# Forming the low part of B22 first in the 7-product steps of a fused encoder block, with its product first

## The chip, the cores and the metric

The kernel runs on one core of a Trainium2 chip. The metric is the device time of one execution in microseconds (us), as the median of several runs. The profile comes from one further execution, whose own time is given beside its span.

## What is computed

The reference is one layer of a streaming encoder block on 256 tokens of width 4096: a normalised input goes through one wide projection, then through a sparse attention branch and a state-space branch, both come back to 4096 columns, are gated, summed, projected once more, normalised and added to the input.

```python
h = rms_norm(x, pre_norm_gain[layer])
proj = h @ w_in[layer]
...
attn = dsa_attention(q, k, v, qi, ki, wi * idx_weight_scale)
y_a = attn.reshape(b, s, ATTN_WIDTH) * jax.nn.silu(gate_a)
...
merged = (gates[:, :, 0, :] * (y_a @ w_branch_attn[layer])
          + gates[:, :, 1, :] * (y_b @ w_branch_ssd[layer]))
out = merged @ w_out[layer]
x = x + rms_norm(out, post_norm_gain[layer])
```

Nearly all the work is in the matrix products with `w_in`, the two branch weights and `w_out`, and nearly all of these go through one function, `pair_gemm`.

## The kernel before, in words

**How a product is made.** Every float32 operand is split into a high part (rounded to the type that TensorE multiplies in one pass, `F32R`) and a low part (what the rounding left). One product is then three matmuls into the same PSUM tile: low of the activations with high of the weights, high with low, high with high (`product`, line 554, in this order). The activations are the stationary operand and are split beforehand; the weights are the moving operand and are split as they arrive. ScalarE makes the high part (an activation with Copy), VectorE the low part (a subtraction).

**Steps.** `pair_gemm` makes two blocks of 128 tokens by two blocks of 512 columns. It runs over 16 pairs of 128 rows of weights (8 in the branch projections), and each pair is one step of a plan. A step loads the weight blocks B12 and B22 into `ra` and B11 and B21 into `rb`, each block 128 by 512. A step of kind D or R makes eight block products. A step of kind S makes seven, by sums and differences of blocks in the manner of Strassen: the sums on the side of the activations lie ready in `ext`, those on the side of the weights are formed in the step. A DMA with accumulation (line 601) first adds B11 to the first half of `ra`, which gives T1; VectorE then forms T2 = T1 - B22 in the second half of `ra` (line 622) and T3, T4 in `rb` (line 623), over the blocks that were there.

**What an S step puts on the engines.** ScalarE makes five high parts: B11 and B21 together (line 507, 1024 columns), B22 (line 617), T1 (line 619), T2 (line 507, 512 columns), T3 and T4 together (line 507). VectorE makes the five low parts belonging to them (line 511, 618, 625, 511, 511) and the two sums of lines 622 and 623. TensorE makes 21 matmuls, in the order of products 2, 1, 3, 5, 6, 7, 4: products 2 and 1 use B21 and B11, product 3 uses B22, product 5 uses T1, product 6 T2, products 7 and 4 T3 and T4. A step of kind D or R has two high parts and two low parts of 1024 columns, no sums, and 24 matmuls.

**Buffers.** The high parts of 1024 columns live in a pool of four buffers, the low parts in another of four (`SBUFS = 4`). An S step takes three of each, for B11 and B21 (`wh_...` of line 613 before), for B22 and T1 together, and for T3 and T4; the part of T2 has a single buffer of its own. A step of kind D or R takes two. A new high part waits until TensorE has done the last product that reads what was in its buffer.

**What sets the order.** The code is recorded, and a scheduler then puts each engine's instructions into an order by their place in the code, by readiness as it models it, and by free buffers; it also decides which buffer a tile gets. `tc.keep_in_program_order` pins an instruction among the pinned ones of its engine. Each engine works through its own queue in order. Beside the steps, generators (`aux`) put the work of earlier stages (rotary embedding, attention, convolution, the scan, the merging) between them, a few instructions at each `step(pace)`.

The plans name the S steps: nine of 16 in most stages (`SX`, `SM`), seven in the state-space stage (`SS`), ten in the later gate projections (`SG` = 1, 3, 4, 6, 7, 9, 10, 12, 13, 14). An S step thus follows another one at 3-4, 6-7 and 9-10, and in the late gates also at 12-13 and 13-14.

Of the kernel before, what the change touches and what calls it, by code (L numbers as in the profile page):

```python
# [13 lines left out]
AF = mybir.ActivationFunctionType  # L14
# [3 lines left out]
P = 128  # L18
# [3 lines left out]
NW = 512  # L22
# [26 lines left out]
def fused_block(tc, x, xT, w_qi, w_misc, w_q0, w_qk, w_vg, w_x, w_z, w_gate, w_br, w_out2, w_out,  # L49
                percol, rows, tabs, tris, pgain, out):  # L50
    nc = tc.nc
    V, A, G, T = nc.vector, nc.scalar, nc.gpsimd, nc.tensor
# [11 lines left out]
    def bank(j):  # L64
        return pq.tile([P, NW], F32, tag=f"p{j}", name=f"p{j}")
# [8 lines left out]
    def fbit(ap):  # L74
        return ap.bitcast(F32)
# [44 lines left out]
    def drain(upto=None):  # L120
        while aux and (upto is None or upto in aux):
            step()

    def push(gen):
        aux.append(gen)
        return gen
# [18 lines left out]
    def raw_tile():  # L145
        return rawp.tile([P, HK, NW], F32, tag="raw", name="raw")

    def load_half(raw, chunk, hf, each=False):
        if each:
            for i in range(HK):  # L150
                nc.sync.dma_start(raw[:, i, :], chunk[:, hf * HK + i, :])
        else:
            nc.sync.dma_start(raw, chunk[:, hf * HK:(hf + 1) * HK, :])
# [333 lines left out]
    def form(i, name):  # L487
        n = int(name[1])
        if name[0] == "S":
            n = (3, 0, 1, 2)[n - 1]  # L490
            return ext[i][:, 0, n, :], ext[i][:, 1, n, :]
        if name[0] == "D":
            return ext[i][:, 0, n - 1, :], ext[i][:, 1, n - 1, :]
        tk = slice((n - 1) * P, n * P)
        k = int(name[2]) - 1
        return base[i][:, 0, k, tk], base[i][:, 1, k, tk]

    def split_tiles(n):
        if n == 1:
            return (whp.tile([P, 1, NW], F32R, tag="wh1", bufs=1, name="wh"),  # L500
                    wlp.tile([P, 1, NW], F32R, tag="wl1", bufs=1, name="wl"))
        return (whp.tile([P, n, NW], F32R, tag="wh", name="wh"),
                wlp.tile([P, n, NW], F32R, tag="wl", name="wl"))

    def split(src, n, sign=1):
        h, l = split_tiles(n)
        A.activation(h, src, AF.Copy, scale=float(sign))  # L507
        if sign < 0:
            V.scalar_tensor_tensor(l, src, -1.0, fbit(h), ALU.mult, ALU.subtract)  # L509
        else:  # L510
            V.tensor_sub(l, src, fbit(h))  # L511
        return [(h[:, j, :], l[:, j, :]) for j in range(n)]
# [16 lines left out]
    def run_pending():  # L529
        while pending:  # L530
            pending.pop(0)()
# [4 lines left out]
    def pair_gemm(what, mode, chunk, plan, outs, evac, hooks={}, pace=1):  # L536

        while len(live) > 1:
            drain(live.popleft())
        left = {}  # L540
        for _, kind in plan:
            for j, n in USES[kind].items():
                left[j] = left.get(j, 0) + n
        ps = {}
        dest = []

        def product(j, i, name, w):
            (ah, al), (bh, bl) = form(i, name), w
            first = j not in ps
            if first:  # L550
                ps[j] = bank(phys[j])
            left[j] -= 1
            for n, (l, r) in enumerate(((al, bh), (ah, bl), (ah, bh))):
                T.matmul(ps[j], l, r, start=first and n == 0, stop=left[j] == 0 and n == 2)  # L554

        def early():
            dest.extend(outs())
            A.activation(dest[0], ps[1], AF.Copy)
            V.tensor_add(dest[1], ps[6], dest[0])
            V.tensor_add(dest[2], ps[7], dest[1])  # L560

        def late():
            if not dest:
                dest.extend(outs())
                A.activation(dest[1], ps[5], AF.Copy, scale=-1.0)
                return
            V.tensor_add(dest[1], ps[5], dest[1])
            if 8 in ended:
                V.tensor_sub(dest[3], dest[3], ps[5])
                return  # L570
            V.scalar_tensor_tensor(dest[3], ps[5], -1.0, dest[2], ALU.mult, ALU.subtract)

        def rest():
            c11, c12, c21, c22 = dest
            if 1 not in ps:
                A.activation(c11, ps[2], AF.Copy)
                A.activation(c21, ps[4], AF.Copy)
                V.tensor_sub(c22, c12, ps[8])
                V.tensor_sub(c12, c12, ps[3])
                return  # L580
            V.scalar_tensor_tensor(c12, ps[3], -1.0, c12, ALU.mult, ALU.subtract)
            if 8 in ps and 8 not in ended:
                V.tensor_sub(c22, c22, ps[8])
            V.tensor_add(c11, ps[2], c11)
            V.tensor_add(c21, ps[4], c21)

        def end():
            rest()
            live.append(push(evac(dest)))

        after = max([n for n, (_, kind) in enumerate(plan) if kind == "S"], default=-2) + 1
        ended = []
        loaded = deque()

        def fetch(n):
            i, kind = plan[n]
            ra, rb = raw_tile(), raw_tile()
            load_half(ra, chunk(i), 0)
            load_half(rb, chunk(i), 1)
            if kind == "S":  # L600
                nc.gpsimd.dma_start(ra[:, 0, :], chunk(i)[:, HK, :], accum_op=ALU.add)
            loaded.append((ra, rb))

        for n in range(LEAD):
            fetch(n)
        for n, (i, kind) in enumerate(plan):
            if n + LEAD < len(plan):
                fetch(n + LEAD)
            ra, rb = loaded.popleft()
            if n in hooks:  # L610
                hooks[n]()
            assert kind_of[i] == what, (n, i, kind_of, len(aux))
            assert kind == "R" or ext_n[i] == {"S": 4, "D": 2}[kind], (n, i, ext_n)
            if kind == "S":
                b11, b21 = split(rb, 2)
                h, l = split_tiles(2)
                A.activation(h[:, 1, :], ra[:, 1, :], AF.Copy)  # L617
                V.tensor_sub(l[:, 1, :], ra[:, 1, :], fbit(h[:, 1, :]))  # L618
                A.activation(h[:, 0, :], ra[:, 0, :], AF.Copy)  # L619
                if n == 1:  # L620
                    run_pending()
                V.tensor_sub(ra[:, 1, :], ra[:, 0, :], ra[:, 1, :])  # L622
                V.tensor_sub(rb, rb, ra[:, 1:2, :].to_broadcast([P, 2, NW]))  # L623
                tc.keep_in_program_order(
                    V.tensor_sub(l[:, 0, :], ra[:, 0, :], fbit(h[:, 0, :])))  # L625
                t1, b22 = ((h[:, j, :], l[:, j, :]) for j in range(2))
                t2, = split(ra[:, 1:2, :], 1)
                t3, t4 = split(rb, 2)
                now = {1: ("A11", b11), 2: ("A12", b21), 3: ("S4", b22), 4: ("A22", t4),
                       5: ("S1", t1), 6: ("S2", t2), 7: ("S3", t3)}  # L630
                for j in (2, 1, 3, 5, 6, 7, 4):
                    product(j, i, *now[j])
            else:
                w = {}
                w[1, 2], w[2, 2] = split(ra, 2, -1)
                w[1, 1], w[2, 1] = split(rb, 2)
                if n == 0 and len(pending) > 1 and turned[0] == "aux":
                    pending.pop(0)()
                if n == 1:
                    run_pending()  # L640
                if n == after:
                    early()
                    if not left.get(5):
                        late()
                        ended.append(5)
                if n == len(plan) - 1 and dest and not ended and left.get(8) == 0:
                    V.scalar_tensor_tensor(dest[3], dest[2], -1.0, ps[8], ALU.mult, ALU.subtract)
                    ended.append(8)
                todo = [(k, j) for j in ((5, 3, 2, 4) if kind == "D" else (3, 8, 2, 4))
                        for k in (1, 2)]  # L650
                for k, j in todo:
                    name = {2: f"A1{k}", 4: f"A2{k}", 8: f"A2{k}", 5: f"A2{k}",
                            3: f"D{k}" if kind == "D" else f"A1{k}"}[j]
                    product(j, i, name, w[k, 1 if j in (2, 4) else 2])
                    if (k, j) == todo[3]:
                        step(pace)
            step(pace)
        if 5 not in ended:
            pending.append(late)
        pending.append(end)  # L660
        turn(mode)
# [714 lines left out]
```

## Time and profile before

| | |
|---|---|
| median of 3 runs | 2809.67 us (2809.47 to 2812.0) |
| profiled execution: its own time / its span | 2809.73 us / 2808.0 us |
| DVE (VectorE) busy | 2508.4 us, 89% |
| ACT (ScalarE) busy | 1803.2 us, 64% |
| POOL (GpSimd) busy | 220.4 us, 8% |
| S steps (instructions of line 622) | 219 |
| matmuls of line 554 | 10095 |

In the rows of the profile, PE is TensorE's matmul, PEld its weight load, DVE VectorE, ACT ScalarE. A row of the timeline gives start and length in us, engine, line, operation, what is written and read, shapes and count; in brackets stands the idle time of the engine before it and what ended that. Starts are what the argument goes by: instructions that follow each other on one engine overlap at their ends.

### The profile page before, as it was taken

How to read it: one execution, taken by the hardware profiler on the slowest of the kernel's cores; microseconds unless marked ns; L12 is line 12 of the kernel's file. 1: busy time of each engine (PE TensorE's matmuls, PEld its weight loads, DVE VectorE, ACT ScalarE, POOL GpSimd, SP SyncE). 2: the span in 40 equal slices, each digit the busy share in tenths (PEclk: the TensorE clock that was granted, in tenths of full speed). 3: DMA queues.
4: the chain of work that ended last, by engine and by line, in shares of the span. 5: the costliest groups of instructions: out<-in, count | busy, mean ns of one | idle time of the engine just before them, and what ended most of it. 6: DMA issues, size and time to landing. Idle time of an engine off the chain costs nothing.

```text
span 2808.0 us, 36830 instructions
## 1 busy us (share of the span) xinstructions
PE 2782.5 (99%) x12603; PEld 2282.5 (81%) x12603; DVE 2508.4 (89%) x3316; ACT 1803.2 (64%) x2541; POOL 220.4 (8%) x263
## 2 busy tenths in 40 slices
PE   9999999999999999999999999999999999999998
PEld 7877888888888888787888788888888888788886
DVE  7668999999999988989898999999987999989975
ACT  7444566665666666887788866666665655655653
POOL 0100000000000000000000010110110100000000
PEclk9999999999999999999999999999999999999999
DMA  9544777777777777576767788888877888867874
GB/s 375 195 168 143 217 225 228 236 210 222 232 224 232 222 219 231 175 222 202 218 195 211 232 256 251 254 251 255 269 257 246 256 268 270 273 215 235 268 258 142
DMA packets 206333, 649.91 MB, mean 231 GB/s; under 512 B 23232, under 2 KB 24000, under 8 KB 206144
## 3 DMA queue, kind: packets, MB, share of 16 engines
q1 hardware_dynamic: 163728, 567.05, 59.9%
q0 software_dynamic: 33776, 64.77, 13.1%
q10 hardware_dynamic: 8640, 15.73, 1.5%
q8 instruction: 99, 1.62, 0.2%
q14 instruction: 90, 0.74, 0.1%
HBM read 627.53 MB, written 19.92 MB: 231 GB/s over the span
## 4 chain that ended last, share of the span: by engine, by line
PE 93%; DVE 4%; ACT 1%; issue 1%; DMA 0%; SPq 0%; DVEq 0%; ACTq 0%
PE p L554 77%; PE p L205 4%; PE p L206 4%; PE p L207 4%; PE p L377 1%; DVE wl L511 1%; ACT wh L507 1%; DVE raw L623 0%; PE p L408 0%; PE p L921 0%; PE p L786 0%; PE p L753 0%; DVE cacc L857 0%; DVE raw L622 0%; DVE og L1255 0%
## 5 line engine op out<-in xcount | busy, mean ns | idle before, releaser
L507 ACT ACTIVATE wh<-raw 128x1024 fp32r<-128x1024 f32 (+1 forms) x1115 | 1056.6, 972 | 594.5 <-DVE raw L622 251.0
L554 PE MATMUL p<-wh,b 128*128 128x512 f32 x4350 | 1431.8, 393 | 0.6 <-ACT wh L507 0.5
L511 DVE TENSOR_TENSOR wl<-raw,wh 128x1024 fp32r<-128x1024 f32 (+1 forms) x886 | 950.5, 1088 | 69.0 <-ACT wh L507 60.7
L554 PEld LDWEIGHTS p<-wh,b 128*128 128x128 f32 x4350 | 816.6, 188 | 170.6 <-ACT wh L507 3.6
L554 PE MATMUL p<-wl,b 128*128 128x512 f32 x2175 | 848.8, 390 | 0.0
L554 PE MATMUL p<-wh,ext 128*128 128x512 f32 x2380 | 796.8, 390 | 1.5 <-ACT wh L507 1.0
L554 PEld LDWEIGHTS p<-wh,ext 128*128 128x128 f32 x2380 | 446.9, 188 | 94.2 <-ACT wh L507 2.9
L554 PEld LDWEIGHTS p<-wl,b 128*128 128x128 f32 x2175 | 408.8, 188 | 82.6 <-DVE wl L509 0.4
L554 PE MATMUL p<-wl,ext 128*128 128x512 f32 x1190 | 469.1, 394 | 3.6 <-DVE wl L625 3.4
L509 DVE SCALAR_TENSOR_TENSOR wl<-raw,wh 128x1024 fp32r<-128x1024 f32 x229 | 279.1, 1219 | 45.9 <-ACT wh L507 44.9
L554 PEld LDWEIGHTS p<-wl,ext 128*128 128x128 f32 x1190 | 223.4, 188 | 63.3 <-DVE wl L625 11.1
L623 DVE TENSOR_TENSOR raw<-raw 128x1024 f32<-128x1024 f32 x219 | 267.9, 1223 | 5.7
L197 DVE TENSOR_TENSOR wl<-raw,wh 128x1024 fp32r<-128x1024 f32 x112 | 139.8, 1249 | 86.2 <-ACT wh L196 86.0
L617 ACT ACTIVATE wh<-raw 128x512 fp32r<-128x512 f32 x219 | 137.7, 629 | 109.7 <-PE p L554 99.4
L196 ACT ACTIVATE wh<-raw 128x1024 fp32r<-128x1024 f32 x112 | 118.4, 1059 | 136.1 <-PE p L207 119.4
L205 PE MATMUL p<-wh,b 128*128 128x512 f32 x512 | 201.9, 395 | 1.7 <-ACT wh L193 1.7
L206 PE MATMUL p<-wl,b 128*128 128x512 f32 x512 | 200.1, 391 | 0.2 <-DVE wl L194 0.2
L207 PE MATMUL p<-wh,b 128*128 128x512 f32 x512 | 199.8, 391 | 0.0
L618 DVE TENSOR_TENSOR wl<-raw,wh 128x512 fp32r<-128x512 f32 x219 | 150.2, 686 | 18.5 <-ACT wh L617 17.0
L622 DVE TENSOR_TENSOR raw<-raw 128x512 f32<-128x512 f32 x219 | 150.8, 689 | 4.9
L625 DVE TENSOR_TENSOR wl<-raw,wh 128x512 fp32r<-128x512 f32 x219 | 149.7, 684 | 0.0
L619 ACT ACTIVATE wh<-raw 128x512 fp32r<-128x512 f32 x219 | 135.2, 617 | 2.8 <-ACT yraw L381 2.7
(242 smaller groups left out, 1839.2 us busy)
## 6 DMA issues: line engine op xcount, KB each, us to landing
raw<-w_gate_d SPq DMA_DIRECT2D x256, 512.0 KB, 5.8
raw<-w_vg_d SPq DMA_DIRECT2D x128, 512.0 KB, 5.3
raw<-w_x_d SPq DMA_DIRECT2D x128, 512.0 KB, 5.1
raw<-w_br_d SPq DMA_DIRECT2D x128, 512.0 KB, 5.4
raw<-w_out_d SPq DMA_DIRECT2D x128, 512.0 KB, 5.1
raw<-w_qk_d SPq DMA_DIRECT2D x96, 512.0 KB, 5.5
raw<-w_z_d SPq DMA_DIRECT2D x64, 512.0 KB, 5.2
raw<-w_qi_d SPq DMA_DIRECT2D x62, 512.0 KB, 7.7
```

The source lines that it names most:

```text
L197: V.tensor_sub(wl, rs, wh.bitcast(F32))
L205: T.matmul(ps[t], al[:, tk], wh[:, i, :], start=first, stop=False)
L206: T.matmul(ps[t], ah[:, tk], wl[:, i, :], start=False, stop=False)
L207: T.matmul(ps[t], ah[:, tk], wh[:, i, :], start=False, stop=last)
L507: A.activation(h, src, AF.Copy, scale=float(sign))
L509: V.scalar_tensor_tensor(l, src, -1.0, fbit(h), ALU.mult, ALU.subtract)
L511: V.tensor_sub(l, src, fbit(h))
L554: T.matmul(ps[j], l, r, start=first and n == 0, stop=left[j] == 0 and n == 2)
L618: V.tensor_sub(l[:, 1, :], ra[:, 1, :], fbit(h[:, 1, :]))
L622: V.tensor_sub(ra[:, 1, :], ra[:, 0, :], ra[:, 1, :])
L623: V.tensor_sub(rb, rb, ra[:, 1:2, :].to_broadcast([P, 2, NW]))
L625: V.tensor_sub(l[:, 0, :], ra[:, 0, :], fbit(h[:, 0, :])))
```

## The change

In an S step the tiles for B22 and T1 are taken before those for B11 and B21. The high part of B22 and its low part (line 619 now) come first, then the high and low part of B11 and B21 (lines 618 and 620), and then, as before, the sums (625, 627), the low part of T1 (629), of T2 (633), of T3 and T4 (511). Six of VectorE's instructions of the step are pinned where one was: all but the low parts of B22 and of T3 and T4. The products run in the order 3, 2, 1, 5, 6, 7, 4: the product with B22 comes first. Nothing is added or left out: the same five high parts, five low parts, two sums and 21 matmuls.

```diff
             if kind == "S":
-                b11, b21 = split(rb, 2)
                 h, l = split_tiles(2)
+                hb, lb = split_tiles(2)
                 A.activation(h[:, 1, :], ra[:, 1, :], AF.Copy)
+                A.activation(hb, rb, AF.Copy)
                 V.tensor_sub(l[:, 1, :], ra[:, 1, :], fbit(h[:, 1, :]))
+                tc.keep_in_program_order(V.tensor_sub(lb, rb, fbit(hb)))
+                b11, b21 = ((hb[:, j, :], lb[:, j, :]) for j in range(2))
                 A.activation(h[:, 0, :], ra[:, 0, :], AF.Copy)
                 if n == 1:
                     run_pending()
-                V.tensor_sub(ra[:, 1, :], ra[:, 0, :], ra[:, 1, :])
-                V.tensor_sub(rb, rb, ra[:, 1:2, :].to_broadcast([P, 2, NW]))
+                tc.keep_in_program_order(V.tensor_sub(ra[:, 1, :], ra[:, 0, :], ra[:, 1, :]))
+                tc.keep_in_program_order(
+                    V.tensor_sub(rb, rb, ra[:, 1:2, :].to_broadcast([P, 2, NW])))
                 tc.keep_in_program_order(
                     V.tensor_sub(l[:, 0, :], ra[:, 0, :], fbit(h[:, 0, :])))
                 t1, b22 = ((h[:, j, :], l[:, j, :]) for j in range(2))
-                t2, = split(ra[:, 1:2, :], 1)
+                h2, l2 = split_tiles(1)
+                A.activation(h2, ra[:, 1:2, :], AF.Copy)
+                tc.keep_in_program_order(V.tensor_sub(l2, ra[:, 1:2, :], fbit(h2)))
+                t2 = h2[:, 0, :], l2[:, 0, :]
                 t3, t4 = split(rb, 2)
...
-                for j in (2, 1, 3, 5, 6, 7, 4):
+                for j in (3, 2, 1, 5, 6, 7, 4):
                     product(j, i, *now[j])
```

Three places of the order show what moved. All are from one late gate projection, at steps 9 and 10 of its plan: two S steps in a row, followed by step 11 of kind R. The names are those of the tiles: `raw_17204` is `ra` of step 10, `raw_17205` its `rb`; `raw_17241` and `raw_17242` belong to step 11.

First ScalarE, before, from the high part of step 9's T3 and T4 on. Behind each row stand the semaphores that it waits for.

```order
L507 ACTIVATE wh_17261<-raw_17159 128x1024 [waits DVE_49,PE_49,Activation_49]
L507 ACTIVATE wh_17291<-raw_17205 128x1024 [waits DMAHW2_49,PE_49,Activation_49]
L617 ACTIVATE wh_17295<-raw_17204 128x512 [waits DMAHW1_49,PE_49,Activation_49]
L619 ACTIVATE wh_17295<-raw_17204 128x512 [waits DMASW0_49]
L507 ACTIVATE wh_17303<-raw_17204 128x512 [waits DVE_49,PE_49,Activation_49]
L507 ACTIVATE wh_17307<-raw_17205 128x1024 [waits DVE_49]
L507 ACTIVATE wh_17337<-raw_17241 128x1024 [waits DMAHW3_49,PE_49,Activation_49]
```

The same place on ScalarE now:

```order
L507 ACTIVATE wh_17261<-raw_17159 128x1024 [waits DVE_49,PE_49,Activation_49]
L617 ACTIVATE wh_17291<-raw_17204 128x512 [waits DMAHW1_49,PE_49,Activation_49]
L622 ACTIVATE wh_17291<-raw_17204 128x512 [waits DMASW0_49]
L618 ACTIVATE wh_17293<-raw_17205 128x1024 [waits DMAHW2_49,PE_49,Activation_49]
L632 ACTIVATE wh_17303<-raw_17204 128x512 [waits DVE_49,PE_49,Activation_49]
L507 ACTIVATE wh_17307<-raw_17205 128x1024 [waits DVE_49]
L507 ACTIVATE wh_17337<-raw_17241 128x1024 [waits DMAHW3_49,PE_49,Activation_49]
```

The high part of B11 and B21 (`wh_17291` before, `wh_17293` now) went from first to third in the step. Its wait on PE changed its meaning too. Before, its buffer was one that step 8 (kind R) had used, and the B22 tile (`wh_17295`) took over the buffer of step 9's B11 and B21, which is free when product 1 of step 9 has ended. Now the two are exchanged: the B22 tile has the buffer from step 8, and the tile of B11 and B21 takes over that of step 9's B11 and B21.

Second VectorE at the same place, before:

```order
L511 TENSOR_TENSOR wl_17262<-raw_17159,wh_17261 128x1024
L511 TENSOR_TENSOR wl_17292<-raw_17205,wh_17291 128x1024
L618 TENSOR_TENSOR wl_17296<-raw_17204,wh_17295 128x512
L622 TENSOR_TENSOR raw_17204<-raw_17204 128x512
L623 TENSOR_TENSOR raw_17205<-raw_17205,raw_17204 128x1024
L625 TENSOR_TENSOR wl_17296<-raw_17204,wh_17295 128x512
L511 TENSOR_TENSOR wl_17304<-raw_17204,wh_17303 128x512
L511 TENSOR_TENSOR wl_17308<-raw_17205,wh_17307 128x1024
```

And now:

```order
L511 TENSOR_TENSOR wl_17262<-raw_17159,wh_17261 128x1024
L619 TENSOR_TENSOR wl_17292<-raw_17204,wh_17291 128x512
L620 TENSOR_TENSOR wl_17294<-raw_17205,wh_17293 128x1024
L625 TENSOR_TENSOR raw_17204<-raw_17204 128x512
L627 TENSOR_TENSOR raw_17205<-raw_17205,raw_17204 128x1024
L629 TENSOR_TENSOR wl_17292<-raw_17204,wh_17291 128x512
L633 TENSOR_TENSOR wl_17304<-raw_17204,wh_17303 128x512
L511 TENSOR_TENSOR wl_17308<-raw_17205,wh_17307 128x1024
```

Two instructions changed places, and the low part of B11 and B21 now stands directly in front of the first sum.

Third TensorE, now, in step 10 from the last matmul of product 1 on. `p4` collects product 1, `p7` product 5, `p8` product 6, `p3` product 7, `p2` product 4.

```order
L554 MATMUL p4_16921<-wh_17293,b10_88 128x512
L554 MATMUL p7_16925<-wh_17291,ext_2763 128x512
L554 MATMUL p7_16925<-wl_17292,ext_2763 128x512
L554 MATMUL p7_16925<-wh_17291,ext_2763 128x512
L554 MATMUL p8_16929<-wh_17303,ext_2763 128x512
L554 MATMUL p8_16929<-wl_17304,ext_2763 128x512
L554 MATMUL p8_16929<-wh_17303,ext_2763 128x512
L554 MATMUL p3_16933<-wh_17307,ext_2763 128x512
L554 MATMUL p2_16879<-wh_17307,b10_88 128x512
L554 MATMUL p3_16933<-wl_17308,ext_2763 128x512
L554 MATMUL p3_16933<-wh_17307,ext_2763 128x512
L554 MATMUL p2_16879<-wl_17308,b10_88 128x512
```

Before, this stretch began with product 3 in place of the end of product 1, and products 7 and 4 stood three and three; now the first matmul of product 4 has moved in front of the second of product 7. The first nine matmuls of the step (products 3, 2, 1) stand ahead of these rows without interleaving.

## The prediction

> **What bounds the kernel now.** I read the page's busy times first, then the chain that ended last, then stretches of 100 us, then the waits.
>
> ```profile
> PE 2782.5 (99%) x12603; PEld 2282.5 (81%) x12603; DVE 2508.4 (89%) x3316; ACT 1803.2 (64%) x2541; POOL 220.4 (8%) x263
> 1587.82 630.40 PE p L554 x2771
> 1200.00:1300.00 100.00, 98.87 (x457) 80.09 (x456) 90.94 (x140) 85.44 (x146) 6.94 (x8) 1.00 0.67 205
> 1500.00:1600.00 100.00, 98.11 (x456) 80.25 (x456) 92.50 (x145) 83.58 (x134) 7.72 (x10) 1.00 0.70 216
> 1900.00:2000.00 100.00, 100.00 (x441) 82.20 (x441) 98.28 (x112) 65.25 (x84) 11.26 (x13) 1.00 0.86 257
> 2300.00:2400.00 100.00, 99.66 (x451) 80.80 (x450) 98.07 (x120) 61.52 (x88) 8.89 (x11) 1.00 0.84 261
> PEld p L554 <- DVE wl L625: 11.1, 22, 1.2
> PEld p L554 <- DVE wl L511: 7.0, 26, 0.4
> PE p L554 <- DVE wl L625: 3.4, 7, 0.7
> ```
>
> TensorE is busy for 2782.5 of 2808.0 us, so no order of work can win more than the 25.5 us between, and part of those lie at the two ends. The chain has one unbroken piece of 630 us of matmuls: there nothing can be won at all. The window rows (PE, PEld, DVE, ACT, POOL busy, then the granted clock, DMA share, GB/s) show TensorE at its full clock, and VectorE close behind it: 98% busy at 1900 and at 2300. What the change can win are TensorE's waits for low parts, the last three rows: 21.5 us if the rows of the weight load and of the matmul are added, and less in truth, since a late weight load is often still hidden.
>
> What matters more is how far VectorE runs ahead of TensorE where two S steps follow each other. This is such a place in a late gate projection, steps 9 and 10 (the order rows above are from here): VectorE, ScalarE, then TensorE.
>
> ```profile
> 1916.71 3.05 DVE L511 TENSOR_TENSOR wl<-raw,wh 128x512 fp32r<-128x512 f32 x3
> 1919.68 0.68 DVE L618 TENSOR_TENSOR wl<-raw,wh 128x512 fp32r<-128x512 f32 x1
> 1920.39 0.69 DVE L622 TENSOR_TENSOR raw<-raw 128x512 f32<-128x512 f32 x1
> 1921.12 1.23 DVE L623 TENSOR_TENSOR raw<-raw 128x1024 f32<-128x1024 f32 x1
> 1922.26 0.68 DVE L625 TENSOR_TENSOR wl<-raw,wh 128x512 fp32r<-128x512 f32 x1
> 1922.87 1.83 DVE L511 TENSOR_TENSOR wl<-raw,wh 128x512 fp32r<-128x512 f32 x2
> 1924.62 1.22 DVE L509 SCALAR_TENSOR_TENSOR wl<-raw,wh 128x1024 fp32r<-128x1024 f32 x1
> 1916.31 2.06 ACT L507 ACTIVATE wh<-raw 128x1024 fp32r<-128x1024 f32 x2 [0.71 <-DVE raw L623]
> 1918.66 0.63 ACT L617 ACTIVATE wh<-raw 128x512 fp32r<-128x512 f32 x1 [0.30 <-PE p L554]
> 1922.38 3.91 ACT L507 ACTIVATE wh<-raw 128x1024 fp32r<-128x1024 f32 x4 [0.54 <-DVE raw L623]
> 1917.28 0.39 PE L554 MATMUL p<-wl,b 128*128 128x512 f32 x1
> 1918.19 0.39 PE L554 MATMUL p<-wh,b 128*128 128x512 f32 x1
> 1922.04 0.39 PE L554 MATMUL p<-wl,b 128*128 128x512 f32 x1
> ```
>
> The first and last PE row are the second matmuls of steps 9 and 10: 4.76 us for 21 matmuls, 0.227 each, so step 9 starts at 1917.05, which I call T. VectorE needs more than that for an S step: from L622 of 1920.39 on, 0.73 + 1.14 + 0.61 + 0.60 + 1.15 to the start of L509, and 1.14 and 0.71 for the two ahead of it, about 6.1 us. It gains this back in steps of kind D or R (24 matmuls, 5.44 us, against two low parts). The bracket of L617 is the row of interest: the high part of B22 of step 10 waited for TensorE, because its buffer was held until product 1 of step 9, the second in the order, had issued its last matmul (1918.19); ScalarE started 0.47 after that. VectorE didn't notice, since it was busy until 1919.68.
>
> **The change part by part.** The number and size of all instructions stay; nothing is priced for work added. The DMAs and their queues are not moved either; the accumulating DMA of an S step must only have landed before line 622 as before.
>
> *Product order and low part of B22 in a step after one of kind D or R.* Product 3 needs its low part 0.6 us earlier than that of B11 and B21 was needed, and gets it so; the latter now comes 0.6 later and is needed 0.68 later. I take nothing. T1's low part is wanted at the same tenth place, after the same work.
>
> *The spacing on VectorE.* L618 to L622 is 0.71, though a subtraction that waits for nothing follows after 0.60 (L625 to L511: 1922.26 to 1922.87 is 0.61): L622 overwrites what L618 reads and waits for its end. Now line 620 stands between, so some 0.11 us per S step goes. Counted over 219 steps that would be 24 us of VectorE, but TensorE only sees it where it waits for VectorE. These are the 22 + 7 waits for L625 in the rows above; at 0.11 each, 3 us. Bounds: nothing, and 8 us if the time adds up over two or three steps. **I take -3.**
>
> By the Trainium skill, "VectorE: DVE Perf Modes", section "The DRAIN you can't avoid", each operation waits until the one before has left the pipe, and a semaphore between them costs nothing extra; by that rule these 3 us would not come, and the sum would be 3 us higher. The rows of this trace (0.61 without a wait, 0.71 with one) speak against it here, and the page's next section itself allows the earlier start.
>
> *The buffer of B11 and B21 where S follows S.* This is the term that decides. Now this tile, not the one of B22, takes over the buffer that product 1 of the step before holds, and product 1 has become the third: its last matmul starts at T + 8 x 0.227 = T + 1.81, before it was T + 1.14. From there, with the rows above:
> - ScalarE starts the high part 0.47 later, T + 2.28; it takes 1.06, and VectorE follows 0.03 behind (h of T3 and T4 starts at 1922.38 and its low part, the second of the pair from 1922.87, at 1924.70 - 1.23 = 1923.47: 1.09). Low part of B11 and B21 from T + 3.37.
> - Line 625 comes 1.14 later, 627 another 0.73 (L622 to L623): T + 5.24.
> - The high part of T3 and T4 starts 1.26 after that (1921.12 to 1922.38), its low part 1.09 later, T + 7.59, and ends after 1.23 at T + 8.82; TensorE needs 0.06 more, T + 8.88.
> - TensorE wants it in step 10 at its 18th matmul, by the order above: T + 4.76 + 17 x 0.227 = T + 8.62. **It comes 0.26 us late.** T1's low part (T + 5.24 + 1.14 + 0.68 + 0.06 = T + 7.12) is wanted at T + 7.03, 0.09 late, which is contained in the 0.26.
>
> Before, the same sum from T + 1.14 has only a high part of 0.63 and one short low part in front of L622, and ends 1.5 us sooner. VectorE now idles too: it would be ready for the low part at about T + 2.1 (1918.54 and one 0.60) and gets it at T + 3.37, 1.3 us lost per pair, which is behind it in the queue for all that follows.
>
> What a late low part costs beyond its lateness is seen at the one place where this gate projection has one before, step 14, third in its row of S steps:
>
> ```profile
> 1943.17 0.68 DVE L625 TENSOR_TENSOR wl<-raw,wh 128x512 fp32r<-128x512 f32 x1
> 1943.35 0.61 PE L554 MATMUL p<-wh,ext 128*128 128x512 f32 x2
> 1943.91 0.50 PE L554 MATMUL p<-wl,ext 128*128 128x512 f32 x1
> 1944.24 0.62 PE L554 MATMUL p<-wh,ext 128*128 128x512 f32 x2
> ```
>
> The second of the pair from 1943.35 starts at 1943.58; the next should start at 1943.81, starts at 1943.91, 0.06 after L625's end, and the one behind it only 0.33 later: another 0.10.
>
> The count is from the changed order. S follows S 66 times. In 29 pairs TensorE's order is the one above, with nothing of `aux` between: 29 x 0.27 (0.26 and rounding) = 7.8. In 22 others, nearly all in the attention stage, one or two instructions of `aux` stand on VectorE inside this stretch (0.1 to 0.6 us each); the same sum gives 0.27 to 0.48, once 1.1, together 9.8. In 15 the scheduler put enough matmuls ahead to cover it: 0. To this come 51 x 0.10 for the restart, 5.1. In the third of three S steps (4 times) VectorE is behind by its own work: its 6.1 us against 4.76, after two idle stretches, make T1's low part about 0.8 late where the rows above lose 0.2, 4 x 0.6 = 2.4.
>
> **The sum:** 7.8 + 9.8 + 5.1 + 2.4 - 3 = +22.1 us. The profiled execution took 2809.73 (span 2808.0 and 1.7 around it), the median is 2809.67; so **2832 us**, 0.8% slower.
>
> The bounds of the main term: if the links from ScalarE to TensorE are 0.26 shorter in all, pairs without `aux` cost nothing, and the sum is about 22 x 0.2 - 3, under +2. If the interleaved matmul of product 4 doesn't help and the rows pay two restarts each, 51 x 0.23 + 5 are added, +38; with VectorE's idle 1.3 us only half made good in the stretches where it is 98% busy (24 pairs x 0.2), +43.
>
> **The rivals.**
> - *The gate is late, but hidden* (no change). The 0.26 is a small difference of long sums, and TensorE's order bends round late operands. For it: in 15 pairs the order already covers it. Against: the same latencies hold to 0.05 in each row looked at. Result about 2809 to 2814.
> - *VectorE's waits go and TensorE with them* (faster). Place: L625's waits, 1100 to 1600 and 2200 to 2400 us. Price: 0.11 per S step on VectorE, up to 8 us off, 2802. It decides if ScalarE's start after the gate comes before VectorE has arrived, that is if VectorE is behind by more than 1.3 us at most pairs; in the row of steps 9 and 10 it isn't.
> - *VectorE becomes the bound in the gates* (much slower). At 98% it has 1.7 us free per 100 and five pairs per gate projection would take up to 6.5 of some 80. If TensorE's own stalls don't loosen the gate again, 4 gates x 5 more and the branch stage give about 2855.
> - *The change does not do what it says*: the order rows show that it does.
>
> **How the numbers follow.** The forecast, slower by 10 to 40 us, has 0.72; much slower 0.08; no change 0.15; faster 0.05. The range of 8 in 10 takes the forecast's bounds and part of "hidden": 2809 to 2853. A measurement of this kernel tells about 0.2%, 5.6 us, from no change: slower by more 0.79, within 0.16, faster 0.05.
>
> **What would show it.** In the profile after, ScalarE's line 618 must have a new idle row ended by PE, some 66 times, and VectorE's line 620 an idle row of about 1 us each ended by ScalarE's 618. TensorE must show waits for line 511 and 629 in the gates, and the piece of 630 us of the chain must break up. The start of 625 should follow 620 by 1.14 and the start of 633 629 by 0.60. I am wrong if line 620 hardly waits, or if it waits and TensorE in 1600 to 2200 still makes 441 matmuls per 100 us; and, on the other side, if the loss is in stages without S pairs.

## The result and the profile after

| | before | after |
|---|---|---|
| median of 5 runs | 2809.67 us (2809.47 to 2812.0) | 2839.52 us (2837.67 to 2846.04) |
| ratio | | 1.0106, 95% interval 1.0095 to 1.0117 |
| profiled execution: own time / span | 2809.73 / 2808.0 us | 2846.04 / 2844.3 us |

The changed kernel is 29.9 us slower by the medians. (The median before is the same from five runs as from the three given above.) The profiled execution after is the longest of its five; what is counted in it stands some 6 us above the median.

Three views of the changed kernel answer to those shown of before: the page's busy times, two 100 us windows (PE, PEld, DVE, ACT, POOL busy, granted clock, DMA share, GB/s), and the two longest pieces that are left where the chain of waits had its 630 us.

```profile
PE 2806.2 (99%) x12603; PEld 2277.9 (80%) x12603; DVE 2493.5 (88%) x3316; ACT 1793.6 (63%) x2540; POOL 220.9 (8%) x263
1900.00:2000.00 100.00, 99.54 (x432) 79.52 (x431) 95.37 (x109) 62.85 (x82) 10.42 (x12) 1.00 0.85 251
2300.00:2400.00 100.00, 99.25 (x440) 80.05 (x439) 94.87 (x114) 57.12 (x76) 8.65 (x10) 1.00 0.84 259
1611.45 173.24 PE p L554 x752
2044.69 194.01 PE p L554 x850
```

The same instructions, and TensorE still reads as busy in each window; but it makes 432 matmuls in the window where it made 441. A waiting matmul shows as a longer row (0.50 for 0.39 below), so the count, and not the busy share, tells of the loss. VectorE's share of the windows fell from 98.28 to 95.37 and from 98.07 to 94.87: it is no bound, it waits. (Its busy time over the whole kernel, 2493.5 for 2508.4 us, doesn't tell of this: the lengths of its 3316 rows add up to 2692.3 us for 2693.8 before, and they only overlap more.) The chain's unbroken 630 us are broken. The longest piece left there has 194; it spans the last gate projection, which has no two S steps in a row, and the first two branch projections, which have one such pair.

The waits after (waiting engine and line, what for: us in total, times, longest):

```profile
DVE wl L620 <- ACT wh L618: 89.5, 96, 5.0
ACT wh L618 <- PE p L554: 49.4, 64, 1.6
PEld p L554 <- DVE wl L629: 30.7, 53, 3.4
ACT wh L618 <- ACT wh L622: 27.9, 42, 0.9
PEld p L554 <- DVE wl L511: 16.5, 50, 0.9
```

The gate of the prediction is the fourth row rather than the second. Of the 64 waits of the second row, 61 stand in S steps behind a step of kind D or R; of the 42 of the fourth, 41 stand where S follows S. In the next fence such a row carries the name of line 622, the instruction in front, but 622 ended at 1935.16 and 618 began at 1935.91, 0.47 after the last matmul of product 1. In 57 of the 66 pairs line 618 starts 0.43 to 0.48 after that matmul: this is the gate. VectorE waits behind line 618 in 96 steps, 0.93 us each; 46 of them, with 40.7 of the 89.5 us, are pairs. TensorE in turn waits for T1's low part (629) and for that of T3 and T4 (511). This is the timeline of steps 9 and 10 in the same late gate projection as in the prediction, T = 1933.63: first ScalarE, then VectorE, then TensorE.

```profile
1934.02 0.62 ACT L617 ACTIVATE wh<-raw 128x512 fp32r<-128x512 f32 x1
1934.54 0.62 ACT L622 ACTIVATE wh<-raw 128x512 fp32r<-128x512 f32 x1
1935.91 1.06 ACT L618 ACTIVATE wh<-raw 128x1024 fp32r<-128x1024 f32 x1 [0.76 <-ACT wh L622]
...
1935.30 0.68 DVE L619 TENSOR_TENSOR wl<-raw,wh 128x512 fp32r<-128x512 f32 x1
1937.01 1.22 DVE L620 TENSOR_TENSOR wl<-raw,wh 128x1024 fp32r<-128x1024 f32 x1 [1.03 <-ACT wh L618]
1938.15 0.68 DVE L625 TENSOR_TENSOR raw<-raw 128x512 f32<-128x512 f32 x1
1938.87 1.22 DVE L627 TENSOR_TENSOR raw<-raw 128x1024 f32<-128x1024 f32 x1
1940.01 0.68 DVE L629 TENSOR_TENSOR wl<-raw,wh 128x512 fp32r<-128x512 f32 x1
1940.61 0.68 DVE L633 TENSOR_TENSOR wl<-raw,wh 128x512 fp32r<-128x512 f32 x1
1941.22 1.23 DVE L511 TENSOR_TENSOR wl<-raw,wh 128x1024 fp32r<-128x1024 f32 x1
...
1935.44 0.39 PE L554 MATMUL p<-wh,b 128*128 128x512 f32 x1
...
1940.43 0.39 PE L554 MATMUL p<-wh,ext 128*128 128x512 f32 x1
1940.75 0.50 PE L554 MATMUL p<-wl,ext 128*128 128x512 f32 x1
1941.09 0.63 PE L554 MATMUL p<-wh,ext 128*128 128x512 f32 x2
...
1942.25 0.39 PE L554 MATMUL p<-wh,b 128*128 128x512 f32 x1
1942.50 0.50 PE L554 MATMUL p<-wl,ext 128*128 128x512 f32 x1
1942.84 0.39 PE L554 MATMUL p<-wh,ext 128*128 128x512 f32 x1
```

The last matmul of product 1 (the row of 1935.44) releases the buffer, and the links follow one by one. The start of the rows of 1940.75 and 1941.09 comes 0.32 and 0.34 after the row ahead of each, for 0.23 without a wait: 0.09 late for T1's low part, then 0.11 to restart. The same again at T3 and T4's low part, 0.25 and 0.34, that is 0.02 and 0.11. The pair loses 0.33 us.

Where the time went, from the start of the same-numbered matmul in both traces (after minus before, profiled executions): the first 315 us +1.5, attention +3.8, state space +4.6, gate projections (the former 630 us) +10.2, branch projections +12.5, last projection +3.8, together 36.3. By the kind of step, from the first matmul of each step to that of the next: the 66 S steps that follow an S step lose 24.7, the 153 S steps behind one of kind D or R 11.1 (10.7 of it in four of them), and the steps of kind D and R gain 1.0. By the kind of loss, about: gaps of up to 0.5 us between matmuls +18.2, longer single waits +13.2, matmuls at half clock +3.5, the first stage +1.5.

The longer waits are few. The longest stands in the branch stage, and what ScalarE waits for there is not the gate (ScalarE, VectorE, TensorE):

```profile
2269.81 0.63 ACT L622 ACTIVATE wh<-raw 128x512 fp32r<-128x512 f32 x1 [5.70 <-DMA raw<-w_br_d]
2270.35 1.04 ACT L618 ACTIVATE wh<-raw 128x1024 fp32r<-128x1024 f32 x1
...
2271.43 1.23 DVE L620 TENSOR_TENSOR wl<-raw,wh 128x1024 fp32r<-128x1024 f32 x1 [4.96 <-ACT wh L618]
...
2277.44 0.50 PE L554 MATMUL p<-wl,ext 128*128 128x512 f32 x1 [2.93 <-DVE wl L629]
```

T1's high part (622) waited 5.70 us for its accumulating DMA, and line 618, whose data were there, stood behind it in ScalarE's queue, as the order rows of the change show it. In the changed kernel 622 stands ahead of 618 in 156 of the 219 S steps; before, T1's high part came after that of B11 and B21.

### The profile page after: what moved, and what is told of

It reads as the page before. It is cut to its first block, busy times and chain, and to the rows that moved or that the text cites. A ratio compares the mean times of both kernels' runs of the same rounds, so it can differ in the third digit from the quotient of the medians.

```text
span 2844.3 us, 36779 instructions
## 1 busy us (share of the span) xinstructions
PE 2806.2 (99%) x12603; PEld 2277.9 (80%) x12603; DVE 2493.5 (88%) x3316; ACT 1793.6 (63%) x2540; POOL 220.9 (8%) x263
## 4 chain that ended last, share of the span: by engine, by line
PE 82%; DVE 9%; issue 4%; DMA 2%; ACT 2%; SPq 0%; POOL 0%; DVEq 0%; ACTq 0%; POOLq 0%
PE p L554 67%; PE p L205 4%; PE p L206 4%; PE p L207 4%; DVE raw L627 2%; DVE wl L620 1%; DVE raw L625 1%; DVE wl L629 1%; DMA raw<-w_br_d 1%; ACT wh L618 1%; DVE wl L633 1%; DVE wl L511 1%; PE p L377 1%; PE p L408 0%; DVE wl L619 0%
## 5 line engine op out<-in xcount | busy, mean ns | idle before, releaser
L554 PE MATMUL p<-wh,b 128*128 128x512 f32 x4350 | 1454.0, 392 | 0.3 <-ACT wh L507 0.2
L507 ACT ACTIVATE wh<-raw 128x1024 fp32r<-128x1024 f32 x677 | 693.8, 1055 | 248.8 <-DVE raw L627 128.7
L554 PE MATMUL p<-wh,ext 128*128 128x512 f32 x2380 | 841.0, 393 | 3.3 <-ACT wh L507 2.6
L511 DVE TENSOR_TENSOR wl<-raw,wh 128x1024 fp32r<-128x1024 f32 x448 | 547.4, 1222 | 67.6 <-ACT wh L507 65.7
L554 PE MATMUL p<-wl,ext 128*128 128x512 f32 x1190 | 478.5, 402 | 12.5 <-DVE wl L629 11.3
L620 DVE TENSOR_TENSOR wl<-raw,wh 128x1024 fp32r<-128x1024 f32 x219 | 267.5, 1222 | 90.4 <-ACT wh L618 89.5
L618 ACT ACTIVATE wh<-raw 128x1024 fp32r<-128x1024 f32 x219 | 231.5, 1057 | 92.7 <-PE p L554 49.4
L197 DVE TENSOR_TENSOR wl<-raw,wh 128x1024 fp32r<-128x1024 f32 x112 | 139.8, 1249 | 86.2 <-ACT wh L196 86.0
L205 PE MATMUL p<-wh,b 128*128 128x512 f32 x512 | 202.3, 396 | 2.1 <-ACT wh L193 2.1
L196 ACT ACTIVATE wh<-raw 128x1024 fp32r<-128x1024 f32 x112 | 118.4, 1059 | 135.7 <-PE p L207 120.9
L207 PE MATMUL p<-wh,b 128*128 128x512 f32 x512 | 200.5, 392 | 0.0
L619 DVE TENSOR_TENSOR wl<-raw,wh 128x512 fp32r<-128x512 f32 x219 | 149.8, 684 | 12.7 <-ACT wh L617 12.2
```

The lines of the kernel that those rows point to most:

```text
L197: V.tensor_sub(wl, rs, wh.bitcast(F32))
L205: T.matmul(ps[t], al[:, tk], wh[:, i, :], start=first, stop=False)
L207: T.matmul(ps[t], ah[:, tk], wh[:, i, :], start=False, stop=last)
L618: A.activation(hb, rb, AF.Copy)
L620: tc.keep_in_program_order(V.tensor_sub(lb, rb, fbit(hb)))
```

## The experiments

Two theories were put against others. **G**, the gate: the loss is the buffer that line 618 waits for. **B**: it is T1's high part in front of line 618 on ScalarE. Each kernel was timed beside the kernel before; its median in the three batches was 2810.07 (e1 to e4), 2811.05 (e5 to e8) and 2810.76 us (e9 to e12).

### e1 and e2: formation and product order apart

In e1 only the order of products is undone, in e2 only that is done, on the kernel before:

```diff
-                for j in (3, 2, 1, 5, 6, 7, 4):
+                for j in (2, 1, 3, 5, 6, 7, 4):
```

```diff
-                for j in (2, 1, 3, 5, 6, 7, 4):
+                for j in (3, 2, 1, 5, 6, 7, 4):
```

> The new way of forming the parts is kept, and only the order of the products is put back to 2, 1, 3, 5, 6, 7, 4. Theory G (the buffer gate: the high part of B11 and B21 waits for product 1 of the S step before): product 1 issues its last matmul at T + 1.14 in place of T + 1.81, the low part of T3 and T4 is there at T + 8.20 and is wanted at T + 8.62, so the loss at pairs of S steps goes. Time 2806 to 2815 us; ScalarE's line 618 still waits for TensorE, but TensorE no longer waits for lines 629 and 511 in the gate projections. Rival B (the loss of the branch stage, 12 us in the profile, comes from T1's high part standing ahead of line 618 on ScalarE and waiting for the accumulating DMA, whatever the order of the products): 2819 to 2824. Rival F (the new formation costs VectorE or ScalarE time everywhere): within 4 us of 2839.

> The old way of forming the parts, and only the products in the new order 3, 2, 1, 5, 6, 7, 4. Theory G: the buffer that product 1 holds goes here to the small high part of B22, so from T + 1.81 only 0.63 of ScalarE and 0.6 of VectorE come before the subtraction, the low part of T3 and T4 ends at about T + 8.0, 0.6 ahead of need, and pairs of S steps lose nothing; in an S step behind one of kind D or R the low part of B22 is now wanted first and is formed second, which costs at most a few us. Time 2808 to 2818. Rival O (the product order alone does it): 2832 to 2842.

Measured: e1 2812.78 us, ratio 1.0009 (1.0000 to 1.0018); e2 2812.87 us, ratio 1.0008 (0.9999 to 1.0017). Either half alone costs at most 5 us, and the two together 30. Theory G is the one that has this: the new formation puts the large high part on the gate, and the new product order moves the gate by 0.68 us; one without the other leaves the low parts in time. These are the window and the waits of e1:

```profile
1900.00:2000.00 100.00, 99.99 (x439) 81.86 (x438) 97.16 (x112) 63.68 (x82) 10.40 (x12) 1.00 0.86 257
ACT wh L618 <- PE p L554: 58.4, 68, 1.6
DVE wl L620 <- ACT wh L618: 81.9, 97, 3.0
PE p L554 <- DVE wl L629: 2.9, 4, 0.8
```

The totals hardly differ from the changed kernel's; the pairs do. There too line 618 starts 0.43 to 0.48 after product 1's last matmul, in 53 of 66, but VectorE waits behind it for 21.0 us in place of 40.7, and the pairs lose 4.2 us against the kernel before in place of 24.7: the wait costs almost nothing while it ends 0.68 earlier. With these two runs F and O fall, and B as a cause that doesn't need the product order: in e1 T1's high part stands ahead of line 618 in 190 of the 219 steps, more than in the changed kernel.

### e3 and e4: the order on ScalarE, and the holds on VectorE

In e3 the two high parts are held in the order of the code; in e4 the four new holds are gone (two are shown).

```diff
-                A.activation(hb, rb, AF.Copy)
+                tc.keep_in_program_order(A.activation(hb, rb, AF.Copy))
...
-                A.activation(h[:, 0, :], ra[:, 0, :], AF.Copy)
+                tc.keep_in_program_order(A.activation(h[:, 0, :], ra[:, 0, :], AF.Copy))
```

```diff
-                tc.keep_in_program_order(V.tensor_sub(lb, rb, fbit(hb)))
+                V.tensor_sub(lb, rb, fbit(hb))
...
-                tc.keep_in_program_order(V.tensor_sub(l2, ra[:, 1:2, :], fbit(h2)))
+                V.tensor_sub(l2, ra[:, 1:2, :], fbit(h2))
```

> The changed kernel, and on ScalarE the high part of B11 and B21 (line 618) is held ahead of T1's high part (line 622), which waits for the accumulating DMA. Theory G with B as its smaller part: the gate projections lose their 10 us as before, the branch stage loses less than its 12; time 2830 to 2837. If B is most of the loss: below 2825. If the order on ScalarE plays no part: within 2 us of 2839.5.

> The changed kernel without the four new holds of VectorE's order (lines 620, 625, 627 and 633; that of line 629 was there before); formation and product order are as in the change. Theory G: the gate is at the same matmul in all 66 pairs, so the loss stays, 2832 to 2842. Rival H (the held order keeps VectorE from doing other work while line 620 waits, and that is the loss): 2808 to 2820.

Measured: e3 2840.33 us, ratio 1.0107 (1.0093 to 1.0121); e4 2833.43 us, 1.0082 (1.0069 to 1.0096). e3 did not bring what G with B expected, it came out as for an order that plays no part: the wait at 2277 is gone from its trace, the pairs lose 24.7 us as before, and the median is unchanged. Whether the order matters once the gate is gone is the question of e9 to e11. e4 is inside G's range, some 6 us under the changed kernel, with intervals that just overlap: the holds are a small part at most, and not the cause.

### e5 to e8: the gate alone, removed and deepened

A fifth buffer for high parts fits only where the raw loads have seven buffers and not eight. So e5 is the changed kernel with seven (the control), e6 has the fifth buffer besides, and e8 is the kernel before with both edits of e6. Formation, product order and holds stay in e5 and e6. In e7, on the changed kernel, T2's parts go into the common pools, which then have four tiles per S step.

```diff
-RBUFS = 8
+RBUFS = 7
...
-    whp = root(tc.tile_pool(name="whp", bufs=SBUFS))
+    whp = root(tc.tile_pool(name="whp", bufs=SBUFS + 1))
```

```diff
         if n == 1:
-            return (whp.tile([P, 1, NW], F32R, tag="wh1", bufs=1, name="wh"),
-                    wlp.tile([P, 1, NW], F32R, tag="wl1", bufs=1, name="wl"))
+            h, l = split_tiles(2)
+            return h[:, 0:1, :], l[:, 0:1, :]
```

> The changed kernel with seven buffers for raw loads in place of eight; control for the next run, which needs the space. All theories: the loads come somewhat later, 2838 to 2850 us; below 2836 no theory explains it.

> The changed kernel, products in the order 3, 2, 1, 5, 6, 7, 4, with seven raw buffers and a fifth buffer for high parts alone; low parts keep four. Theory G: line 618 finds a free buffer and is done before VectorE arrives; the low part's buffer is released at T + 1.81 as before, where VectorE is busy until about T + 2.1, so line 620 starts some 1.3 us earlier than now and the pairs' loss goes. Time 2806 to 2818 if the control stands at 2840, otherwise 22 to 32 under the control. Rival I (formation and product order together are wrong for another reason, a low part wanted earlier than VectorE's order makes it): within 5 us of the control.

> The changed kernel with T2's parts in the pool of the others, so that four tiles per step share four buffers: the buffer that line 618 takes is released at T + 2.49 (by product 5) in place of T + 1.81, 0.68 later. Theory G: line 620 from T + 4.05, the low part of T1 0.77 late and that of T3 and T4 0.94 late in a pair, 0.6 to 0.7 us more than now in 51 pairs and some of it in the other 15: 2865 to 2890 us. Rival I, and the theory that lateness at the gate is only a sign of something else: 2835 to 2845.

> The kernel before with seven raw buffers and the fifth buffer for high parts. Theory G: its gate at T + 1.14 was hidden already, so nothing is gained: 2808 to 2816. Were the buffer a gain whatever the formation, it would be below 2804, and the run with it would say nothing on the change.

Measured: e5 2854.77 us, 1.0156 (1.0142 to 1.0170); e6 2829.77, 1.0065 (1.0052 to 1.0077); e7 2883.73, 1.0259 (1.0245 to 1.0273); e8 2808.83, 0.9993 (0.9984 to 1.0002). The control moved by 15 us, more than expected. Against it the fifth buffer brings 25.0 us, inside the 22 to 32 of theory G; in the traces the loss of the 66 pairs goes from 24.3 to 2.7. In the kernel before the buffer brings nothing. e7 falls into G's range too, but by another way than I had written: ScalarE already waits at the high part of B22, and line 618 comes after it in the queue. Steps 9 and 10 of the same gate projection in e7, T = 1962.22:

```profile
1964.51 0.63 ACT L617 ACTIVATE wh<-raw 128x512 fp32r<-128x512 f32 x1 [0.98 <-PE p L554]
1965.05 0.62 ACT L622 ACTIVATE wh<-raw 128x512 fp32r<-128x512 f32 x1
1965.57 1.04 ACT L618 ACTIVATE wh<-raw 128x1024 fp32r<-128x1024 f32 x1
...
1966.64 1.22 DVE L620 TENSOR_TENSOR wl<-raw,wh 128x1024 fp32r<-128x1024 f32 x1 [0.78 <-ACT wh L618]
```

Line 620 starts at T + 4.42, 1.04 later than in the changed kernel, not 0.68. More buffer pressure is more loss, but e7 doesn't measure the price of one later gate.

e6 still stood 20 us over the kernel before, with no gate in the way. The waits of its trace:

```profile
ACT wh L622 <- DMA raw<-w_gate_d: 35.2, 14, 6.5
ACT wh L622 <- DMA raw<-w_br_d: 23.8, 5, 5.2
ACT wh L622 <- DMA raw<-w_out_d: 11.7, 3, 6.0
PEld p L554 <- DVE wl L629: 19.5, 24, 2.1
```

With seven raw buffers the accumulating DMAs come later (T1's high part waits 15.4 us for them in the changed kernel, 46.0 in e5), and here they hold it up for 88.6 us in all, in front of line 618: theory B.

### e9 to e12: what is left without the gate

e9 is e6 with e3's hold on ScalarE, e10 is e6 without the new holds on VectorE (as in e4), e11 is e5 with the hold on ScalarE, e12 is e1 without the new holds on VectorE. The edits are those shown above.

> The kernel of the fifth high buffer (2829.8 us, still 20 over the kernel before) with line 618 held ahead of T1's high part (line 622) on ScalarE. In its trace T1's high part stood ahead of line 618 in 108 of 219 steps and waited 88 us for accumulating DMAs, and line 620 behind it. Theory G plus B (once the gate is gone, what is left is ScalarE's order): 2806 to 2816 us. If B is nothing, as it was with the gate in place: 2827 to 2833.

> The kernel of the fifth high buffer without the four new holds of VectorE's order; ScalarE's order is the scheduler's, T1's high part ahead of line 618 in 110 of 219 steps. Theory B: the loss stays for the most part, 2820 to 2832. Rival H (the held order on VectorE keeps other work behind a waiting line 620): 2806 to 2814.

> The control with seven raw buffers and four high buffers (2854.8 us) with line 618 held ahead of line 622. If its 15 us over the changed kernel come from T1's high part waiting for later DMAs in front of line 618: 2838 to 2846. If they come from the loads themselves, at whatever waits for them: 2851 to 2857.

> The new formation with the order 2, 1, 3, 5, 6, 7, 4 and without the new holds of VectorE's order: 2809 to 2814 by theory G, as with the holds (2812.8); below 2807 the formation would be a gain once the gate is early and VectorE's order is free.

| | median us | ratio to before | 95% interval |
|---|---|---|---|
| e9 | 2806.31 | 0.9982 | 0.9974 to 0.9991 |
| e10 | 2824.75 | 1.0046 | 1.0033 to 1.0060 |
| e11 | 2840.08 | 1.0102 | 1.0088 to 1.0116 |
| e12 | 2811.23 | 1.0002 | 0.9994 to 1.0011 |

ScalarE's order is worth 23.5 us where the gate is gone (e6 to e9) and 14.7 where the loads are late and the gate is there (e5 to e11): this is the whole of the control's 15 us. Where eight raw buffers have the loads in time, it is worth nothing (e3). So B is a mechanism, but not that of the changed kernel's median: it needs late DMAs. With the order held, the fifth buffer alone brings 33.8 us (e11 to e9). Of this some 25 is the gate: the pairs lose 24.8 in e11's trace and gain 0.7 in e9's. Most of the rest is in S steps behind one of kind D or R, which lose 6.5 and gain 3.1. Without the holds on VectorE e10 is 5 us under e6, much like e4; the intervals overlap, so a cost of the holds is likely and not shown.

e9 is also faster than both kernels, by 0.09 to 0.26% than the one before. The chain's unbroken piece and the count of matmuls are back:

```profile
1588.10 628.63 PE p L554 x2768
1900.00:2000.00 100.00, 100.00 (x441) 82.37 (x440) 96.95 (x112) 64.48 (x83) 10.74 (x13) 1.00 0.87 259
```

## Why the prediction was right, and where it was not

**The sign and the mechanism** were right, and shown: with the gate taken away (e9), or left 0.68 earlier (e1), the loss is gone; with more pressure on the buffers it grows (e7). 29.9 us were measured for 22.1 forecast, inside the range. The four terms of the pairs add up to 25.1 us, and the pairs lost 24.7 in the trace, but term by term this is partly luck, as said below.

**The buffer of B11 and B21 where S follows S.** Link by link the pair of steps 9 and 10 came as worked out: high part at T + 2.28 (forecast 2.28), low part at T + 3.38 (3.37), line 627 at T + 5.24 (5.24), the low part of T3 and T4 at T + 7.59 (7.59). The size was also right, 0.33 us for 0.26 + 0.10, but it falls elsewhere: T1's low part, 0.09 late and "contained in the 0.26", stops TensorE first and costs its own restart, so that T3 and T4's is only 0.02 late. I had counted one restart per pair; there are two, which stood only in the upper bound. That the sizes meet is luck as well.

**The counts.** Pairs with `aux` between, "nearly all in the attention stage", were to cost 9.8 and their restarts 2.2. The 24 pairs of that stage lost 6.1, and its steps of kind D and R gained 3.3 back, so that it grew by 3.8. This term was too large by about a factor of two, and the other 42 pairs lost 18.6 for 13.1 forecast: two errors that cancel. Why the attention pairs lose less was not tried.

**"In 15 pairs the scheduler put enough matmuls ahead"**: nothing here speaks against it; the 15 pairs that lost least lost 0.06 to 0.19 us each. The step behind one of kind D or R ("I take nothing") came out as said where the gate is early: e1 and e2 leave room for at most 5 us each. In the changed kernel these steps lose 11.1 us, nearly all in four of them (at 1274.8, 1552.8, 2271.4 and 2432.7). There TensorE waits for parts of T1 to T4, not for that of B22; these are the long waits below.

**The spacing on VectorE** is there: line 625 follows 620 by 1.14 and 633 follows 629 by 0.60, while 627, which waits for 625, follows by 0.72. By the Trainium skill, "VectorE: DVE Perf Modes", section "The DRAIN you can't avoid", the wait would cost nothing extra; the 0.60 and 0.72 in this trace disagree again. VectorE's busy time fell by 15 us. But the gain of 3 us in TensorE's time is not shown: e1, which has the spacing and hardly a late low part, is not faster than before, and e9 and e8 differ by 2.5 us in medians of two batches, with intervals that overlap. The term stays open.

**What was missing** are the few long waits, about 13 us in the profiled execution, with 3.5 us at half clock behind them. In e3's profile, of 2839.6 us span, the same count gives 9.4 and 4.2. The forecast went pair by pair, and priced an idle stretch of VectorE as regained in the next step of kind D or R. In the branch stage, which has only six pairs, a lag meets other waits: T1's DMA at 2269.81, and this one, where ScalarE's queue has an instruction that waits for a load of an earlier stage's data in front of the high part of T3 and T4 (ScalarE, then TensorE):

```profile
2437.23 0.63 ACT L484 ACTIVATE b<-fr 128x512 fp32r<-128x512 f32 x1 [4.01 <-DMA fr<-mscr]
2437.76 2.94 ACT L507 ACTIVATE wh<-raw 128x1024 fp32r<-128x1024 f32 x3
...
2438.86 0.51 PE L554 MATMUL p<-wh,ext 128*128 128x512 f32 x1 [2.57 <-ACT wh L507]
```

The same pair of rows, with TensorE waiting behind it, is in the traces of e3 (4.29 us), e4 and e5 (3.11 and 3.13, ended there by TensorE and not by the DMA). In e1, e2, e6 and e9, which have no late gate, line 484 waits for such loads too, up to 3.5 to 4.3 us, and TensorE waits for nothing behind it. That the stall follows from the lag is argued from this, not shown by a run of its own. That ScalarE's new order puts T1's high part, and with it a DMA, in front of line 618 stood in the order rows, and I passed over it: "the DMAs and their queues are not moved either" is true, but the engine that waits for them now has more behind it.

**The signs and the rivals.** Line 618 was to have a new idle row ended by PE "some 66 times". The view has 64, but this is a coincidence: 61 of them stand in other steps, and the row of the pairs carries the name of line 622. "Hidden" falls with the 432 matmuls; the 96 waits of line 620 alone would not do it, since e1 has 97. "VectorE becomes the bound in the gates" falls with its 95.37% at 1900, less than before. "VectorE's waits go" falls for this kernel; in e9, without the gate, it may be the sign that was looked for.

## What to carry over

Whoever changes the order in which tiles are formed or consumed also changes which tile inherits which buffer: look up, for each new tile, the last reader of the buffer it takes over, and count from that reader's new place to the next deadline. Two edits that cost nothing each can cost 1% together, so test a bundle by its parts and their combination. A spare buffer tests a gate, if its own cost has a control and the gain is looked for in the gate's own steps; and where loads can be late, an instruction that waits for a DMA belongs behind those on its queue that don't. A count of waits that meets the forecast is not yet the wait that was meant: look in which steps they stand.

## What the hardware showed besides

After some waits TensorE ran at half its clock for about 3.4 us. Three windows of the changed kernel's trace, each just behind a TensorE wait for a part (2.12 us at 1558.12, and the two shown above, 2.93 at 2277.44 and 2.57 at 2438.86); the number behind POOL's is the granted clock:

```profile
1558.60:1562.00 3.40, 3.40 (x11) 2.43 (x10) 3.40 (x6) 2.93 (x5) 0.00 (x0) 0.59 0.53 172
2277.40:2280.80 3.40, 3.36 (x14) 2.50 (x15) 3.40 (x4) 3.40 (x5) 0.00 (x0) 1.00 0.56 175
2439.80:2443.20 3.40, 3.40 (x8) 2.80 (x9) 3.40 (x5) 3.19 (x4) 0.00 (x0) 0.50 0.56 189
```

At a clock of 0.59 and 0.50 the 3.40 us lose 1.4 and 1.7. The longest of the three waits was not followed by a slow clock, and in e3's trace one of 1.24 us was, 1.7 us behind one of 0.77 (0.57 from 1281.1 to 1284.5). By the Trainium skill, "TensorE: Matmul & The Clock Gate", section "HAM oscillation — how this bites in real kernels", idle gaps have to exceed about 3.4 us for this; here shorter ones did, so a single wait of two or three us may cost some 1.5 us beyond itself. Nor does the length of the waits decide alone: the changed kernel's trace has nearly the same two waits as e3's (0.75, then 1.27 to 1280.46), and no slow clock behind them. What decides between the cases is not settled by these runs.
